# Attention scores without rotation from queries and keys in two parts: three float32r passes in place of one float32 product

## The chip, the cores and the metric

The kernel runs on one core of one Trainium2 chip. The metric is the device time of one execution in microseconds (us), the median of three runs. "float32r" below is the type F32R of the code: a four-byte type whose products the kernel uses wherever it carries a number as a coarse part ("hi") plus the rest ("lo").

## The reference

One inference step of four layers: a state-space layer, a pooling layer, a latent-attention layer, and a second state-space layer. The change lies in the attention layer alone. There 384 tokens (128 of the prompt, 256 of the sample) attend with 16 heads; the sample tokens also see 128 cached context tokens. Per head:

```
q_nope, q_pe = split((rmsnorm(q_a) @ wq_b) per head, 128 + 64)
k_nope, v    = split((ckv_n @ wkv_b) per head, 128 + 128)
s = einsum('bqhd,bkhd->bhqk', q_nope, k_nope) + einsum('bqhr,bkr->bhqk', q_pe, k_pe)
p = softmax(s * 192 ** -0.5)
o = einsum('bhqk,bkhd->bqhd', p, v)
```

The first product of `s` (128 features, not rotated) is what the change computes in another way. The second (64 rotated features) stays.

## The kernel before, in words

Nearly all weight products are taken in three float32r passes: both operands are split into hi (a copy rounded to float32r, on ScalarE) and lo (operand minus hi, on VectorE), and hi·hi, hi·lo and lo·hi are added up in one PSUM bank. The helper `split` (L145 to L147) does the two steps on a tile, `unit` (L131) and `unit2` (L776) on weights that arrive by DMA: `whi` and `wlo`. A few products are plain float32, among them both score products and the product of weights and values.

In `mla` (L588) the 16 heads run in a loop (L768 to L773) that is skewed by one head: `scores(h + 1)` is written ahead of `values(h)`. `scores(h)` builds the head's queries (L712 to L714: six passes, 384 columns, into a bank of the pool `acc`) and copies them to SBUF as `qn` on ScalarE (L716); builds its keys (L719 to L721: three passes, 512 columns) and copies them as `kn` on VectorE (L723); then, for three tiles T of 128 queries, takes the unrotated product (L729) and the rotated one (L730) into a bank of the pool `sp`. Tiles 0 and 2 are of the sample and see 384 keys; tile 1 is of the prompt and sees 128. Tile 1 writes the last 128 columns of the bank that holds tile 0. Each tile then gets its maximum (L733), `-scale` times it (L734), the exponential on ScalarE (L735), the reciprocal of its sum (L736) and the product with it (L737), which gives `P`.

`values(h)` transposes P in seven pieces (L752) into two banks, `tp` and `ad`, copies these out as `PT` on ScalarE (L755) and VectorE (L757), multiplies with the values `V` (L762, L763), multiplies with the gate (`pr`), and splits the result into `ph` and `pl`. Every fourth head `vals4` builds V for four heads in twelve passes (L698 to L700). Between the two, `beside()` (L771) splits two weight units of the next layer ahead of time and stores their lo parts to DRAM (L1024): `raw` in, `whi` on ScalarE, `wlo` on VectorE, `lod` out.

The order in which each engine meets its instructions is not that of the code: the Tile framework schedules the recorded instructions by their dependences and its own costs, so an edit in one place can move others. Once built, the order is fixed, and each engine works it off in turn. Tiles of one tag in a pool with `bufs=2` alternate between two buffers; with `bufs=1` the next writer waits for the last reader.

Of the kernel before, what the change touches and what calls it, by code (L numbers as in the profile page):

```python
# [9 lines left out]
F32 = mybir.dt.float32  # L10
F32R = mybir.dt.float32r
# [9 lines left out]
NT = 384  # L21
# [9 lines left out]
class Net:  # L31
# [556 lines left out]
    def mla(self, l, side, end, beside):  # L588
        nc, tc, A = self.nc, self.tc, self.A
        v = nc.vector  # L590
        scale = 192.0 ** -0.5
        with ExitStack() as outer:
# [25 lines left out]
            with tc.tile_pool(name="mp", bufs=1) as mp:  # L618
# [27 lines left out]
                for k in range(4):  # L646
                    ps = self.bank(self.tp, "tp")
# [20 lines left out]
                for n in range(2):  # L668
                    pss = [self.bank(self.acc, "acc") for _ in range(3)]
                    self.prod_b(pss, A["mla_wqp"][n], 1, qh, ql)  # L670
                    for T in range(3):
                        o = qp[:, T, n * 512:(n + 1) * 512]
# [4 lines left out]
                for k in range(8):  # L677
                    ps = self.bank(self.tp, "tp")
# [25 lines left out]
            def scores(h):  # L704
# [5 lines left out]
                for k in range(2):  # L710
# [1 line left out]
                    nc.tensor.matmul(ps, wh[:, c], qh[:, k, :], start=k == 0, stop=False)  # L712
                    nc.tensor.matmul(ps, wh[:, c], ql[:, k, :], start=False, stop=False)
                    nc.tensor.matmul(ps, wl[:, c], qh[:, k, :], start=False, stop=k == 1)  # L714
                qn = wk.tile([128, NT], F32, name="qn", tag="qn")
                nc.scalar.copy(out=qn, in_=ps)  # L716
                ps = self.bank(self.acc, "acc")
                c = slice(w0 + 256, w0 + 384)
                nc.tensor.matmul(ps, wh[:, c], ch, start=True, stop=False)  # L719
                nc.tensor.matmul(ps, wh[:, c], cl, start=False, stop=False)  # L720
                nc.tensor.matmul(ps, wl[:, c], ch, start=False, stop=True)  # L721
                kn = wk.tile([128, 512], F32, name="kn", tag="kn")
                v.tensor_copy(out=kn, in_=ps)  # L723
                hp = slice(64 * (h % 2), 64 * (h % 2) + 64)
                P = wk.tile([128, 3, NT], F32, name="P", tag="P")
                pa, pb = self.bank(self.sp, "sp"), self.bank(self.sp, "sp")
                for T, o, ks in ((0, pa[:, :384], slice(128, 512)), (1, pa[:, 384:], slice(0, 128)), (2, pb[:, :384], slice(128, 512))):
                    ts_ = slice(T * 128, (T + 1) * 128)
                    nc.tensor.matmul(o, qn[:, ts_], kn[:, ks], start=True, stop=False)  # L729
                    nc.tensor.matmul(o, qpT[hp, h // 2, ts_], kpT[hp, ks], start=False, stop=True)  # L730
                    n = ks.stop - ks.start
                    mx = self.work.tile([128, 3], F32, name="mx", tag="mx", bufs=6)
                    v.reduce_max(out=mx[:, 0:1], in_=o, axis=AX.X)  # L733
                    v.tensor_scalar(out=mx[:, 0:1], in0=mx[:, 0:1], scalar1=-scale, scalar2=None, op0=OP.mult)  # L734
                    nc.scalar.activation(out=P[:, T, :n], in_=o, func=AF.Exp, scale=scale, bias=mx[:, 0:1], accum_out=mx[:, 1:2])  # L735
                    v.reciprocal(out=mx[:, 2:3], in_=mx[:, 1:2])  # L736
                    v.tensor_scalar(out=P[:, T, :n], in0=P[:, T, :n], scalar1=mx[:, 2:3], scalar2=None, op0=OP.mult)  # L737
# [796 lines left out]
```

## Time and profile before

| | us |
|---|---|
| median of three runs | 1810.89 (1810.05 to 1817.27) |
| profiled execution | 1812.23 |
| its span, first to last instruction | 1810.4 |
| heads of the attention, 1073 to 1237 us of the span | 164 |

In the profile PE is TensorE with its matmuls, PEld its weight loads, DVE VectorE, ACT ScalarE, SP the engine whose queue issues the DMAs. A float32 product stands in the trace as two matmul rows with two weight loads, a float32r pass as one of each; a row with x2 or x4 merges neighbours. The ends of matmuls are modelled, so the cost of a matmul is read from its start to the start of the next, not from its duration.

### The profile page before, as it was taken

The page shows a single profiled execution, that of the slowest core. Times are in us where ns is not written, and L with a number is a line of the kernel's source. Part 1 is how long each engine was busy: PE and PEld are TensorE (multiplying, and loading weights), DVE is VectorE, ACT ScalarE, POOL GpSimd, SP SyncE. Part 2 cuts the span into 40 slices and gives each one's busy share as a digit, 9 for nine tenths or more (in the row PEclk, how much of TensorE's full clock was granted, in tenths as well). Part 3 has the DMA queues.
Part 4 walks back from the last instruction along what each step waited for, and adds up shares of the span by engine and source line. Part 5 has one row for each costly group of instructions (what it writes and reads, how often), then busy time and mean ns, then how long its engine had stood idle before and what let it go on. Part 6 is the DMA issues. An engine that isn't in the chain of part 4 may idle for free.

```text
span 1810.4 us, 29493 instructions
## 1 busy us (share of the span) xinstructions
PE 1686.1 (93%) x10928; PEld 1318.4 (73%) x10928; DVE 1254.9 (69%) x3149; ACT 978.3 (54%) x1588; POOL 5.4 (0%) x16
## 2 busy tenths in 40 slices
PE   4999999998999998999998999999899999899998
PEld 1464454654799977999887885657678778689986
DVE  7699876787476567888867737763439978656435
ACT  2653487636654455655546555642354777754322
POOL 0000000000000000000000000000000000000000
PEclk7999999997899998999998999999999999799999
DMA  8337767654577664655563566732567754567552
GB/s 311 98 119 240 228 182 220 195 180 137 166 252 231 193 205 135 188 162 163 179 218 113 186 205 229 239 127 82 181 226 226 227 182 140 166 232 213 172 165 72
DMA packets 174831, 334.30 MB, mean 185 GB/s; under 512 B 78528, under 2 KB 101856, under 8 KB 174688
## 3 DMA queue, kind: packets, MB, share of 16 engines
q1 hardware_dynamic: 165728, 319.84, 55.6%
q10 hardware_dynamic: 8960, 12.59, 2.1%
q8 instruction: 86, 1.41, 0.3%
q14 instruction: 57, 0.47, 0.1%
HBM read 279.54 MB, written 52.82 MB: 184 GB/s over the span
## 4 chain that ended last, share of the span: by engine, by line
PE 72%; DVE 9%; ACT 9%; DMA 6%; issue 3%; SPq 0%; ACTq 0%; DVEq 0%
PE acc L175 6%; PE acc L177 6%; PE acc L176 6%; PE sp L1122 4%; PE acc L829 4%; PE acc L830 4%; PE acc L831 4%; PE acc L213 3%; PE acc L159 3%; PE acc L160 3%; PE acc L161 3%; PE acc L204 3%; ACT Eq L1188 3%; DMA adw<-in_ada_w 2%; PE adps L99 2%
## 5 line engine op out<-in xcount | busy, mean ns | idle before, releaser
L51 DVE TENSOR_TENSOR wlo<-raw,whi 128x1024 fp32r<-128x1024 f32 (+2 forms) x234 | 281.2, 1204 | 246.3 <-ACT whi L138 229.0
L138 ACT CAST whi<-raw 128x1024 fp32r<-128x1024 f32 x246 | 257.6, 1050 | 315.2 <-PE acc L177 130.0
L51 DVE TENSOR_TENSOR Pr<-E,Tb 128x256 f32<-128x256 f32 (+1 forms) x504 | 173.9, 354 | 9.3 <-ACT E L1131 3.3
L159 PE MATMUL acc<-hh,whi 128*128 128x384 f32 x512 | 177.3, 347 | 0.2
L161 PE MATMUL acc<-hh,wlo 128*128 128x384 f32 x512 | 174.3, 340 | 0.3 <-DVE wlo L51 0.2
L160 PE MATMUL acc<-hl,whi 128*128 128x384 f32 x512 | 174.3, 340 | 0.0
L829 PE MATMUL acc<-y,whi 128*128 128x384 f32 x448 | 152.7, 345 | 8.1 <-ACT y L146 5.8
L831 PE MATMUL acc<-y,wlo 128*128 128x384 f32 x448 | 152.0, 340 | 1.0 <-DVE wlo L51 1.0
L830 PE MATMUL acc<-y,whi 128*128 128x384 f32 x448 | 152.7, 342 | 0.1
L175 PE MATMUL acc<-whi,ph 128*128 128x512 f32 x384 | 152.5, 397 | 0.0
L176 PE MATMUL acc<-wlo,ph 128*128 128x512 f32 x384 | 151.4, 394 | 0.0
L177 PE MATMUL acc<-whi,pl 128*128 128x512 f32 x384 | 151.3, 394 | 0.0
L51 DVE TENSOR_TENSOR E<-R,E 128x128 f32<-128x128 f32 (+1 forms) x504 | 123.1, 254 | 31.5 <-ACT E L1125 25.2
L51 DVE TENSOR_TENSOR R<-Pr 128x128 f32<-128x128 f32 (+1 forms) x504 | 123.7, 255 | 5.8
L159 PEld LDWEIGHTS acc<-hh,whi 128*128 128x128 f32 x512 | 97.1, 190 | 5.2 <-issue 2.0
L204 PE MATMUL acc<-h,raw 128*128 128x384 f32 x256 | 98.8, 516 | 0.0
L161 PEld LDWEIGHTS acc<-hh,wlo 128*128 128x128 f32 x512 | 96.8, 189 | 2.1 <-DVE wlo L51 0.9
L160 PEld LDWEIGHTS acc<-hl,whi 128*128 128x128 f32 x512 | 97.1, 190 | 1.0 <-issue 0.3
L99 PE MATMUL adps<-adw,scond 128*32 128x256 f32 x768 | 70.6, 422 | 27.7 <-DMA adw<-in_ada_w 27.3
L213 PE MATMUL acc<-raw,h 128*128 128x512 f32 x192 | 95.8, 617 | 0.0
L829 PEld LDWEIGHTS acc<-y,whi 128*128 128x128 f32 x448 | 84.6, 190 | 11.6 <-ACT y L146 7.1
L831 PEld LDWEIGHTS acc<-y,wlo 128*128 128x128 f32 x448 | 84.9, 190 | 2.2 <-DVE wlo L51 1.6
(285 smaller groups left out, 3261.6 us busy)
## 6 DMA issues: line engine op xcount, KB each, us to landing
adw<-in_ada_w SPq DMA_DIRECT2D x96, 512.0 KB
raw<-in_s_glu SPq DMA_DIRECT2D x64, 512.0 KB
raw<-in_s_wu SPq DMA_DIRECT2D x48, 512.0 KB
raw<-in_s_wz SPq DMA_DIRECT2D x40, 512.0 KB
raw<-in_s_wo SPq DMA_DIRECT2D x32, 512.0 KB
yq<-yd SPq DMA_DIRECT2D x64, 192.0 KB
lod<-wlo SPq DMA_DIRECT2D x24, 512.0 KB
wlo<-lod SPq DMA_DIRECT2D x24, 512.0 KB
```

The costliest lines, as they stand in the source:

```text
L51: return self.nc.vector.tensor_tensor(out=out, in0=a, in1=b, op=op)
L138: nc.scalar.copy(out=hi, in_=raw)
L159: nc.tensor.matmul(ps, h, xh[:, kk, :ncol], start=i == 0, stop=False)
L160: nc.tensor.matmul(ps, h, xl[:, kk, :ncol], start=False, stop=False)
L161: nc.tensor.matmul(ps, l, xh[:, kk, :ncol], start=False, stop=i == n - 1)
L175: nc.tensor.matmul(ps, xh[:, kk, xs], h, start=kk == 0, stop=False)
L176: nc.tensor.matmul(ps, xh[:, kk, xs], l, start=False, stop=False)
L177: nc.tensor.matmul(ps, xl[:, kk, xs], h, start=False, stop=kk == 2 * nu - 1)
L204: self.nc.tensor.matmul(ps, w[:, k * 128:(k + 1) * 128], x[:, k, :], start=k == 0, stop=k == 7)
L829: self.nc.tensor.matmul(ps, h, y[:, 0, k], start=u == 0 and k == 0, stop=False)
L830: self.nc.tensor.matmul(ps, h, y[:, 1, k], start=False, stop=False)
L831: self.nc.tensor.matmul(ps, l, y[:, 0, k], start=False, stop=u == 1 and k == 7)
```

## The change

`qn` and `kn` become pairs of float32r tiles, made by `split`: hi on ScalarE, lo on VectorE, both read from the PSUM bank. The unrotated product of each tile is three passes, each with a weight load of its own; the rotated product stays float32. The four tiles have one buffer each, where `qn` and `kn` had two. The lines behind the edit move by two (L733 becomes L735, and so on); the two copies now appear under the helper's lines, L146 and L51.

```diff
-                qn = wk.tile([128, NT], F32, name="qn", tag="qn")
-                nc.scalar.copy(out=qn, in_=ps)
+                qn = [wk.tile([128, NT], F32R, name="qn", tag=f"qn{i}", bufs=1) for i in range(2)]
+                self.split(*qn, ps)
...
-                kn = wk.tile([128, 512], F32, name="kn", tag="kn")
-                v.tensor_copy(out=kn, in_=ps)
+                kn = [wk.tile([128, 512], F32R, name="kn", tag=f"kn{i}", bufs=1) for i in range(2)]
+                self.split(*kn, ps)
...
-                    nc.tensor.matmul(o, qn[:, ts_], kn[:, ks], start=True, stop=False)
+                    nc.tensor.matmul(o, qn[0][:, ts_], kn[0][:, ks], start=True, stop=False)
+                    nc.tensor.matmul(o, qn[0][:, ts_], kn[1][:, ks], start=False, stop=False)
+                    nc.tensor.matmul(o, qn[1][:, ts_], kn[0][:, ks], start=False, stop=False)
                     nc.tensor.matmul(o, qpT[hp, h // 2, ts_], kpT[hp, ks], start=False, stop=True)
```

The scheduler orders the attention anew; outside it the engines' orders are as before. Two places matter. The first is TensorE in head 3 (the heads counted from 0), from the end of its keys on. Before:

```order
L721 MATMUL acc<-ch,wlo 128x512
L752 MATMUL tp<-ident,P 128x128
L752 MATMUL ad<-ident,P 128x128
L729 MATMUL sp<-kn,qn 128x384
L730 MATMUL sp<-kpT,qpT 128x384
L729 MATMUL sp<-kn,qn 128x384
L730 MATMUL sp<-kpT,qpT 128x384
L752 MATMUL tp<-ident,P 128x128 x3
L752 MATMUL ad<-ident,P 128x128 x2
L762 MATMUL acc<-PT,V 128x2x128 x2
```

With the change, the same place (L729 to L731 are the three passes, L732 the rotated product, L754 the transposes, L764 the product with the values):

```order
L721 MATMUL acc<-ch,wlo 128x512
L754 MATMUL tp<-ident,P 128x128
L754 MATMUL ad<-ident,P 128x128
L729 MATMUL sp<-kn,qn 128x384 x2
L754 MATMUL tp<-ident,P 128x128 x3
L754 MATMUL ad<-ident,P 128x128 x2
L730 MATMUL sp<-kn,qn 128x384
L731 MATMUL sp<-kn,qn 128x384
L732 MATMUL sp<-kpT,qpT 128x384
```

The hi·hi passes of tiles 0 and 2 now stand together, the last five transposes have moved in front of the other passes, and the product with the values comes after the second group of L730 to L732 instead of right behind the transposes.

The second place is VectorE in the same head, around the copy of the keys. Before:

```order
L737 TENSOR_SCALAR P<-P,mx 128x128
L51 TENSOR_TENSOR pl<-pr,ph 128x384
L723 COPY kn<-acc 128x512
L736 RECIPROCAL mx<-mx 128x1
L51 TENSOR_TENSOR wlo<-raw,whi 128x1024
L737 TENSOR_SCALAR P<-P,mx 128x384
```

With the change:

```order
L739 TENSOR_SCALAR P<-P,mx 128x128
L51 TENSOR_TENSOR qn<-acc,qn 128x384
L51 TENSOR_TENSOR wlo<-raw,whi 128x1024
L738 RECIPROCAL mx<-mx 128x1
L51 TENSOR_TENSOR pl<-pr,ph 128x384
L739 TENSOR_SCALAR P<-P,mx 128x384
L51 TENSOR_TENSOR kn<-acc,kn 128x512
```

In this head the lo part of the keys stands behind a weight split of 1024 columns (`wlo`), which before came after the copy of the keys.

## Rows read from the trace of the kernel before

**Rows 1.** The page, busy time and share of the span of each engine.

```profile
PE 1686.1 (93%) x10928; PEld 1318.4 (73%) x10928; DVE 1254.9 (69%) x3149; ACT 978.3 (54%) x1588; POOL 5.4 (0%) x16
```

**Rows 2.** Busy time by stretch: all heads; head 3; a head with vals4. Columns as headed.

```profile
core 0: us, PE busy (x) PEld busy (x) DVE busy (x) ACT busy (x) POOL busy (x), PEclk, DMA share, GB/s
1073.00:1237.00 164.00, 150.47 (x625) 97.31 (x624) 118.00 (x291) 91.22 (x197) 0.00 (x0) 0.99 0.58 192
...
1100.75:1110.53 9.78, 8.66 (x39) 5.46 (x38) 7.96 (x18) 5.28 (x12) 0.00 (x0) 1.00 0.61 194
...
1119.86:1132.42 12.56, 11.77 (x52) 7.81 (x51) 9.01 (x23) 9.44 (x20) 0.00 (x0) 1.00 0.40 126
```

**Rows 3.** Timeline of TensorE through head 3: start, duration, instruction [idle before].

```profile
1102.33 0.40 PE L721 MATMUL acc<-ch,wlo 128*128 128x512 f32 x1
1102.57 0.27 PE L752 MATMUL tp<-ident,P 128*128 128x128 f32 x1
1102.68 0.27 PE L752 MATMUL ad<-ident,P 128*128 128x128 f32 x1
1103.61 0.88 PE L729 MATMUL sp<-kn,qn 128*128 128x384 f32 x2 [0.66 <-DVE mx L736]
1104.42 0.91 PE L730 MATMUL sp<-kpT,qpT 64*128 64x384 f32 x2
1105.26 0.91 PE L729 MATMUL sp<-kn,qn 128*128 128x384 f32 x2
1106.10 0.91 PE L730 MATMUL sp<-kpT,qpT 64*128 64x384 f32 x2
1106.94 0.55 PE L752 MATMUL tp<-ident,P 128*128 128x128 f32 x3
1107.32 0.38 PE L752 MATMUL ad<-ident,P 128*128 128x128 f32 x2
1108.16 1.13 PE L762 MATMUL acc<-PT,V 128*128 128x256 f32 x4 [0.46 <-ACT PT L755]
1109.13 0.38 PE L729 MATMUL sp<-kn,qn 128*128 128x128 f32 x2
1109.44 0.49 PE L730 MATMUL sp<-kpT,qpT 64*128 64x128 f32 x2
...
1110.53 0.42 PE L712 MATMUL acc<-qh,whi 128*128 128x384 f32 x1
1110.79 0.34 PE L713 MATMUL acc<-ql,whi 128*128 128x384 f32 x1
1110.96 0.34 PE L714 MATMUL acc<-qh,wlo 128*128 128x384 f32 x1
```

**Rows 4.** Groups of VectorE's instructions, 1072 to 1238 us: busy, mean ns | idle before.

```profile
L51 DVE TENSOR_TENSOR wlo<-raw,whi 128x1024 fp32r<-128x1024 f32 x26 | 31.7, 1218 | 4.9 <-ACT whi L138 2.8 <-PE acc L161 2.1
L723 DVE COPY kn<-acc 128x512 f32<-128x512 f32 x16 | 11.0, 688 | 3.6 <-PE acc L721 3.6
L51 DVE TENSOR_TENSOR pr<-acc,sz 128x384 f32<-128x384 f32 x16 | 8.9, 554 | 5.1 <-PE acc L763 4.8
L51 DVE TENSOR_TENSOR wlo<-raw,whi 128x512 fp32r<-128x512 f32 x4 | 2.7, 682 | 0.0
```

**Rows 5.** Groups of ScalarE's instructions, the same stretch.

```profile
L755 ACT COPY PT<-tp 128x512 f32<-128x512 f32 x16 | 9.4, 589 | 8.7 <-PE tp L752 8.7
L716 ACT COPY qn<-acc 128x384 f32<-128x384 f32 x16 | 7.6, 476 | 4.9 <-PE acc L714 4.8
```

**Rows 6.** Who TensorE waited for, 1072 to 1238 us: total, times, longest.

```profile
PE sp L729 <- DVE mx L736: 4.0, 6, 0.7
...
PE acc L762 <- ACT PT L755: 2.8, 6, 0.5
```

**Rows 7.** Timeline of VectorE in head 3, around the copy of the keys.

```profile
1102.77 0.69 DVE L723 COPY kn<-acc 128x512 f32<-128x512 f32 x1
...
1103.44 1.21 DVE L51 TENSOR_TENSOR wlo<-raw,whi 128x1024 fp32r<-128x1024 f32 x1
1104.57 0.42 DVE L737 TENSOR_SCALAR P<-P,mx 128x384 f32<-128x384 f32 x1
```

## The prediction, on record before the changed kernel ran

> **What bounds the kernel now.** First the page: TensorE is busy 93% of the span, no other engine over 69% [rows 1]. That is an average of four layers; the change touches only the loop over heads, so next the busy time by stretch. The loop takes 164 us, in which PE is busy 150.5, DVE 118.0, ACT 91.2, at a granted clock of 0.99, which is the higher level, 2.4 GHz [rows 2]. PE is the bound there, but not without gaps, and VectorE is the runner-up.
>
> Then one head in the timeline [rows 3]; by start to start it gives every price. A float32r pass over 384 columns takes 0.17 us behind another such pass (1110.79 to 1110.96), but 0.26 when a float32 product stands before it (1110.53 to 1110.79): changing from float32 to float32r costs 0.09. A float32 score product over 384 columns takes 0.81 (1103.61 to 1104.42) or 0.84 (1105.26 to 1106.10), one over 128 columns 0.31 (1109.13 to 1109.44). A transpose takes 0.11 (1102.57 to 1102.68). The head has two gaps. Between the second transpose, whose time is over by about 1102.8, and 1103.61 PE waits some 0.8 us. The row names a DVE reciprocal; what stands in DVE just before that is the copy of the keys, 1102.77 to 1103.46 [rows 7], and that is what L729 needs. The second gap is 0.46 at L762: the transposes have only just been done, and their copy PT takes 0.59 on ACT [rows 3, 5]. The waits summed over the loop show the same two, 4.0 and 2.8 us in six heads each [rows 6]; small, because modelled ends of matmuls cover part of each gap.
>
> **The change, part by part.**
>
> *Large tiles.* Two per head, 32 in all: a float32 product of 0.81 and one of 0.84 give way to three passes each at 0.17, 0.51. That saves 0.30 + 0.33 = 0.63 per head, 16 x 0.63 = 10.1 us.
>
> *Small tile.* One per head, 0.31 against three passes over 128 columns, which the trace before does not have. From below a third of the pass over 384, 0.06, from above the transpose of 128 columns, 0.11: 0.18 to 0.33 for three. I take 0.25, nearer to the transpose, since that has the same columns. Saves 0.06, 1.0 us in all (2.1 saved to 0.3 lost).
>
> *Changes of type.* The rotated product stays float32 and sits between the passes, and the scheduler puts transposes between them too. Counted along PE's order, a float32r pass follows a float32 product or a transpose 24 times in the loop before and 72 times after. 48 more at 0.09 [rows 3] cost 4.3 us. From below nothing, where PE stands waiting anyway; from above all of it. I take all.
>
> PE's own work so falls by 10.1 + 1.0 - 4.3 = 6.8 us (between 5.5 and 12.2).
>
> A rule of the skill speaks against the size of the first term. The rows show a float32 product at 0.84, or nearly five passes. The Trainium skill, "FP8 and Floating Point Precision", section TensorE Precision Notes, says that true float32 is four passes through the array. At four passes of 0.17 the product would cost 0.68 and the three passes save one, 32 x 0.17 = 5.4 us instead of 10.1; the sum would be 2.1. The trace disagrees on the time, so the row decides, and the sum is made by it.
>
> *VectorE.* Added: the lo part of the queries, 384 columns from PSUM, by the nearest row (pr) 0.55, 16 x 0.55 = 8.9 us. The lo part of the keys takes the place of the copy of the keys, 0.69 against 0.68 for a subtraction of 512 columns [rows 4]: nothing. DVE comes to 126.9 us in a loop of some 157, 81%. *ScalarE.* The queries' copy stays (0.48); the keys' hi part is new, 512 columns from PSUM as in PT, 0.59, 16 x 0.59 = 9.4 us [rows 5]: 100.6 of 157, 64%. Neither becomes the bound by its sum, so both cost nothing beside a PE that is busy over 90%; what they can cost is lateness.
>
> *The wait for the keys.* Before: end of L721, one DVE copy, L729. After: end of L721, hi on ACT (0.59 against 0.69 for the copy: L729 starts no later), then lo on DVE (0.69) before L730 may start. PE's new order covers that: behind the two L729 (0.26 + 0.17) stand five transposes (5 x 0.11), 0.98 us of work against 0.69. And because the transposes now precede the long passes, PT is copied under the 2.5 us of L730 to L732, and the 0.46 wait at L762 goes. Against that, VectorE works in order. Along its order a weight split of 1.21 us stands between the head's queries and its keys' lo part in 4 of 16 heads (3, 5, 7, 11); in head 3 before, it stood behind the copy and the scaling of P at 1104.57 was late by it, but nobody needed that until 1106.94 [rows 3, 7]. Now the transposes in front of L730 do. Estimate: of the 12 heads without vals4, the nine others gain 0.46 each, 4.1 us; three lose 1.21 - 0.46 = 0.75, 2.3 us; and ACT's queue puts the exponential of tile 2 and the cast of `ph` before the keys' cast in several heads, which I let eat the remaining 1.8. In the heads with vals4 its twelve passes lie beside the split, and only PE's own work counts [rows 2]. So the waits come to 0, between -4.1 and +9.4 (the whole new ACT link open in every head).
>
> *Single buffers.* The cast of the next head's queries must wait until the small tile of this head has been read. In most heads that lies before L712 on PE anyway; where it was moved behind L719, the cast waits about 1 us, but L729 waits for the keys, which come later still. Cost 0, and if it shows, it is inside the +9.4.
>
> *Next layer's weights.* The SP queue issues the same loads and `lod` stores in another order. They are read a layer later; cost 0.
>
> Sum: -6.8. The profiled execution took 1812.2, its span 1810.4, and lies 1.3 above the median of the runs, so on its own count it becomes 1805.4, and in medians 1810.9 - 6.8 = 1804.1.
>
> **The rivals.**
>
> A. *The second link is open.* PE saves 6.8, but the keys' extra link through ACT shows in every head: +9.4, net +2.6, 1813.5. For it: the wait before L729 is there today. Against: the five transposes that now stand in it.
>
> B. *Slower: VectorE's queue ends the wait.* In each of the 12 heads without vals4 the keys' lo part and the scaling of P stand behind a weight split (1.21) on top of the ACT link (0.59): 12 x 1.80 = 21.6, less 6.8, +14.8, 1825.7. It decides from the point at which heads wait 1.0 us more each than today (6.8 + 9.1 over 16). For it: DVE at 81%, strictly in order, 26 such splits in the loop [rows 4]. Against: only 4 heads have the split at that place.
>
> C. *More than the forecast.* The changes of type fall into waits, and PT's wait goes in all 12 heads: -12.2 - 5.5 = -17.7, 1793.2; half of the way there, -12.2, 1798.7. For it: of the 48 added changes some 20 are transposes followed by an L729 that waits for the keys anyway. Against: it wants ACT and DVE on time throughout.
>
> D. *The passes here cost more than 0.17.* If a float32 product is four passes and the rest is the price of the place (short groups, weights of their own for every tile), then three passes cost 0.63 of 0.84 and save 0.21: 32 x 0.21 = 6.7 instead of 10.1, in all -3.4, 1807.5. Against: the groups of six passes at 0.17 have new weights in every pass too. The rule of the Trainium skill above points to this side.
>
> **How the numbers follow.** Forecast 0.48, C 0.20, D 0.12, A 0.13, B 0.07. A measurement of this kernel can tell about 0.5% from no change, 9.1 us. Forecast and D lie within that, between -9 and -2; of the forecast's share I put 0.05 beyond -9, so faster is 0.20 + 0.05 = 0.25. Slower is B, 0.07, and the worst of A, 0.01: 0.08. The rest, 0.67, is within 0.5%. The range reaches down to the half of C, 1798, and up past A to 1815; the rest of C and B, about 2 in 10, is left out.
>
> **What would show each step right or wrong.** The loop over heads should last some 157 us instead of 164, and no other stretch change. L729 to L731 should stand 0.17 apart within a group, 0.26 at its head, and groups of 384 columns end after 0.6 us. L764 should wait for PT in few heads. If the loop is no shorter and PE's waits name the lo part of `kn` or P, A or B has it; then the heads with the weight split in front must be the longest. If the passes lie 0.21 apart, D has it. A gain over 9 us with no wait left at L764 speaks for C. The forecast is wrong if the loop grows, or if the time moves outside the loop.

## The result, and the profile after

The changed kernel takes 1823.68 us (median of 15 runs, 1815.84 to 1834.84) against 1810.05 us (15 runs, 1805.94 to 1817.27) for the kernel before on the same chip: ratio 1.0077, 95% interval 1.0057 to 1.0096. It is slower by some 0.8%, where 1804.1 us had been predicted, with 0.08 on slower. The profiled execution took 1816.74 us (span 1814.9), so it is one of the shorter of the fifteen; the mean granted clock of TensorE in it is 0.962; over the fifteen it goes from 0.969 in the shortest run to 0.950 in the longest.

The page's line of busy times, against [rows 1]: every engine has a little more to do, and TensorE is no less busy.

```profile
PE 1690.2 (93%) x10976; PEld 1329.1 (73%) x10976; DVE 1262.5 (70%) x3165; ACT 986.2 (54%) x1604; POOL 5.4 (0%) x16
```

Busy time by stretch, with the columns of [rows 2]: the loop over heads; 2 us in it in which TensorE waits; the 13.7 us behind that wait.

```profile
1067.30:1239.30 172.00, 157.77 (x675) 110.46 (x673) 125.90 (x307) 99.35 (x213) 0.00 (x0) 0.93 0.54 183
1136.50:1138.50 2.00, 0.50 (x4) 0.17 (x2) 2.00 (x5) 1.91 (x5) 0.00 (x0) 1.00 0.06 22
1138.50:1152.20 13.70, 13.68 (x35) 9.49 (x36) 8.63 (x24) 5.72 (x13) 0.00 (x0) 0.50 0.76 258
```

The loop takes 171.9 us, 7.8 more than the 164.1 of before, and PE is busy 157.8 us instead of 150.5. The granted clock of the loop has fallen from 0.99 to 0.93. The third row shows how: 13.7 us at 0.50, which is the lower level, 1.2 GHz. The clock's record has two such stretches inside the loop, 13.7 us from 1138.5 and 10.2 us from 1182.9, and a third, of 3.4 us, lies over its end; the loop before has only the one at its end. At half speed half of the time is lost: 12.8 us against 1.7.

Ahead of each of the two TensorE had stood still: 1.51 us up to 1138.5 and 2.08 us up to 1183.2. The timeline of TensorE around the first (start, duration, instruction, idle before):

```profile
1136.39 0.40 PE L721 MATMUL acc<-ch,wlo 128*128 128x512 f32 x1
1136.62 0.27 PE L754 MATMUL tp<-ident,P 128*128 128x128 f32 x1
1136.73 0.27 PE L754 MATMUL ad<-ident,P 128*128 128x128 f32 x1
1138.52 1.26 PE L729 MATMUL sp<-kn,qn 128*128 128x384 f32 x2 [1.51 <-ACT kn L146]
1139.58 0.52 PE L730 MATMUL sp<-kn,qn 128*128 128x384 f32 x1
1139.90 0.52 PE L731 MATMUL sp<-kn,qn 128*128 128x384 f32 x1
1140.35 1.65 PE L732 MATMUL sp<-kpT,qpT 64*128 64x384 f32 x2
```

The pass waits for the keys' hi part, `kn` by ScalarE (L146). Behind the wait passes follow each other by 0.32 us (1139.58 to 1139.90) instead of 0.17, and the rotated product takes 1.57 (1140.35 to 1141.92) instead of 0.84. ScalarE's timeline shows why `kn` is late:

```profile
1135.63 0.48 ACT L146 CAST qn<-acc 128x384 fp32r<-128x384 f32 x1 [0.34 <-PE sp L730]
1136.59 1.04 ACT L138 CAST whi<-raw 128x1024 fp32r<-128x1024 f32 x1 [0.48 <-PE acc L720]
1137.54 0.36 ACT L737 ACTIVATE P<-sp,mx 128x128 f32<-128x128 f32 x1
1137.80 0.19 ACT L737 ACTIVATION_READ_ACCUMULATOR P<-sp,mx 128x1 f32 x1
1137.89 0.57 ACT L146 CAST kn<-acc 128x512 fp32r<-128x512 f32 x1
```

The last product of the keys starts at 1136.39, and its cast at 1137.89: a weight cast of 1.04 us and an exponential stand in front of it in an engine that works strictly in order. At 1180.73 the same weight cast stands there again, with two exponentials behind it; the keys' cast starts at 1182.59, and TensorE waits 2.08 us:

```profile
1183.22 0.69 PE L729 MATMUL sp<-kn,qn 128*128 128x384 f32 x1 [2.08 <-ACT kn L146]
```

The waits of the loop, against [rows 6] (total, times, longest):

```profile
PE sp L729 <- ACT kn L146: 6.1, 5, 2.1
PE tp L754 <- DVE P L739: 4.9, 5, 2.2
PE acc L764 <- ACT PT L757: 1.4, 3, 0.5
```

At full clock the passes look as foreseen. The first two tiles of an early head, against [rows 3]:

```profile
1078.22 0.44 PE L729 MATMUL sp<-kn,qn 128*128 128x384 f32 x1
1078.50 0.33 PE L730 MATMUL sp<-kn,qn 128*128 128x384 f32 x1
1078.67 0.34 PE L731 MATMUL sp<-kn,qn 128*128 128x384 f32 x1
1078.94 0.91 PE L732 MATMUL sp<-kpT,qpT 64*128 64x384 f32 x2
1079.78 0.44 PE L729 MATMUL sp<-kn,qn 128*128 128x384 f32 x1
```

Passes are 0.17 apart, but from L729 to the next L729 it is 1.56 us, against 1.65 to 1.68 for two float32 products in [rows 3] (1103.61 to 1105.26, 1104.42 to 1106.10). A tile saves some 0.1 us, not 0.3. On VectorE and ScalarE the new work has the durations and the sum foreseen, against [rows 4, 5]:

```profile
L51 DVE TENSOR_TENSOR kn<-acc,kn 128x512 fp32r<-128x512 f32 x16 | 10.9, 682 | 0.7 <-ACT kn L146 0.7
L51 DVE TENSOR_TENSOR qn<-acc,qn 128x384 fp32r<-128x384 f32 x16 | 8.8, 553 | 1.3 <-ACT qn L146 1.0
```

```profile
L146 ACT CAST kn<-acc 128x512 fp32r<-128x512 f32 x16 | 9.4, 588 | 1.0 <-PE acc L721 1.0
```

### The profile page after: what moved, and what is told of

The parts are those of the page before. It is cut to its first block, busy times and chain, and to the rows that moved or that the text cites. A ratio compares the mean times of both kernels' runs of the same rounds, so it can differ in the third digit from the quotient of the medians.

```text
span 1814.9 us, 29615 instructions
## 1 busy us (share of the span) xinstructions
PE 1690.2 (93%) x10976; PEld 1329.1 (73%) x10976; DVE 1262.5 (70%) x3165; ACT 986.2 (54%) x1604; POOL 5.4 (0%) x16
## 4 chain that ended last, share of the span: by engine, by line
PE 69%; ACT 10%; DVE 9%; DMA 8%; issue 3%; SPq 0%; ACTq 0%; DVEq 0%
PE acc L175 6%; PE acc L177 6%; PE acc L176 6%; PE sp L1124 4%; PE acc L831 4%; PE acc L832 4%; PE acc L833 4%; PE acc L159 3%; PE acc L161 3%; DMA adw<-in_ada_w 3%; PE acc L160 3%; PE acc L213 3%; ACT Eq L1190 3%; PE acc L204 2%; PE adps L99 2%
## 5 line engine op out<-in xcount | busy, mean ns | idle before, releaser
L51 DVE TENSOR_TENSOR wlo<-raw,whi 128x1024 fp32r<-128x1024 f32 (+2 forms) x234 | 281.1, 1204 | 247.2 <-ACT whi L138 232.1
L51 DVE TENSOR_TENSOR Pr<-E,Tb 128x256 f32<-128x256 f32 (+1 forms) x504 | 173.3, 353 | 9.3 <-ACT E L1133 3.3
L51 DVE TENSOR_TENSOR E<-R,E 128x128 f32<-128x128 f32 (+1 forms) x504 | 122.5, 253 | 31.5 <-ACT E L1127 25.2
L51 DVE TENSOR_TENSOR R<-Pr 128x128 f32<-128x128 f32 (+1 forms) x504 | 123.0, 254 | 5.7
```

What stands on the lines that cost most here:

```text
L51: return self.nc.vector.tensor_tensor(out=out, in0=a, in1=b, op=op)
```

## The experiments

The theories, numbered as in the expectations below: 1, the keys' parts wait behind other work in an in-order queue, TensorE stands still, and the clock falls to half; 2, the split's load on VectorE and ScalarE costs by itself; 3, the passes and what stands between them cost more than was counted; 4, the stretches at half clock have nothing to do with the waits. Theory 5 came up on the way. Each kernel was compared with the kernel before on its own chip. "Loop" is from the first query pass of head 0 to the first pass of the output product in the one profiled execution; "lost" is what the lower clock took of it, half of the time at 0.50.

| kernel | median us (runs) | ratio to before [95%] | loop us | lost us | longest wait in the loop, us |
|---|---|---|---|---|---|
| before | 1810.05 (15) | 1 | 164.1 | 1.7 | 1.0 |
| after | 1823.68 (15) | 1.0077 [1.0057, 1.0096] | 171.9 | 12.8 | 2.1 |
| two buffers | 1831.31 (6) | 1.0092 [1.0059, 1.0124] | 167.1 | 6.8 | 2.1 |
| keys on VectorE | 1841.29 (5) | 1.0149 [1.0125, 1.0173] | 196.0 | 30.2 | 2.0 |
| passes only | 1819.55 (11) | 1.0028 [1.0010, 1.0046] | 166.3 | 6.4 | 1.5 |
| split work only | 1823.72 (6) | 1.0052 [1.0033, 1.0071] | 169.8 | 5.1 | 1.6 |
| keys of the head before | 1808.65 (12) | 0.9985 [0.9968, 1.0002] | 159.9 | 1.7 | 1.8 |
| idle filled | 1820.19 (8) | 1.0041 [1.0026, 1.0056] | 172.1 | 0.7 | 1.1 |
| rotated first, three passes | 1812.72 (12) | 1.0004 [0.9987, 1.0022] | 161.9 | 7.8 | 1.6 |
| rotated first, float32 | 1803.14 (6) | 0.9938 [0.9916, 0.9961] | 153.0 | 1.7 | 1.4 |
| keys first, three passes | 1811.12 (12) | 0.9994 [0.9970, 1.0017] | 154.6 | 2.6 | 1.1 |
| keys first, float32 | 1801.17 (7) | 0.9933 [0.9908, 0.9957] | 152.1 | 1.7 | 0.7 |
| before, 128 rows | 1799.86 (6) | 0.9934 [0.9909, 0.9960] | 150.5 | 0.0 | 1.9 |
| after, 128 rows | 1804.35 (11) | 0.9960 [0.9941, 0.9979] | 156.0 | 6.8 | 2.5 |
| before, padded | 1802.96 (7) | 0.9948 [0.9927, 0.9969] | 152.6 | 1.7 | 2.1 |
| keys first, padded, float32 | 1792.25 (6) | 0.9880 [0.9858, 0.9901] | 141.0 | 1.6 | 0.7 |
| keys first, padded, three passes | 1800.10 (6) | 0.9921 [0.9896, 0.9946] | 148.7 | 3.1 | 1.2 |

(The wait before the last head's transposes, 2.1 to 2.7 us at the loop's end in nearly every kernel, is left out of the last column.)

The loop and the loss are those of one execution each; the mean granted clock is on record for every run. (1 - clock) x span is half of the time at 0.50 in a whole execution, the measure of "lost" for all of it. It is 73 us on average for after, and 61 to 63 us for before on the four chips of the experiments (12 to 23 runs each; on the chip of after the clocks of before aren't on record). The 11 to 12 us between them are the 11.1 us between the two profiled loops, and what is left of the time is the same: 1750 us for after, 1750 to 1752 for before. So the clock accounts for what after loses in its runs as a whole, as far as before on those chips stands for before on this one.

One reservation holds for most rows. The scheduler orders the loop anew for each kernel. TensorE keeps its order, instruction by instruction, in the two kernels with 128 rows and in "before, padded", and in "two buffers" but for 16 of 672 places. In "split work only", "passes only", "keys of the head before", "idle filled" and "keys on VectorE" some 250 to 350 of these places hold another instruction, so these kernels show what an edit and its new order do together.

### Two buffers

```
-                qn = [wk.tile([128, NT], F32R, name="qn", tag=f"qn{i}", bufs=1) for i in range(2)]
+                qn = [wk.tile([128, NT], F32R, name="qn", tag=f"qn{i}", bufs=2) for i in range(2)]
...
-                kn = [wk.tile([128, 512], F32R, name="kn", tag=f"kn{i}", bufs=1) for i in range(2)]
+                kn = [wk.tile([128, 512], F32R, name="kn", tag=f"kn{i}", bufs=2 - i) for i in range(2)]
```

> Both parts of the queries and the hi part of the keys get two buffers again (the lo part of the keys stays at one, for space). Theory 1 (long waits for the keys' hi part in ScalarE's queue let TensorE's clock fall to its lower level; buffers have no part in it): as with the change, 1816 to 1830 us, still one or two stretches of the heads' loop at a granted clock of 0.5. Rival 'single buffers' (the next head's cast of the queries waits for the last reader of the old ones, and the keys' cast stands behind it): 1806 to 1813, no such stretch.

No gain: 1.0092 against 1.0077. The order hardly moves and the waits are like those of after: the longest is 2.08 us again, with 13.7 us at half clock behind it; an earlier one, of 1.53 us, has none. The single buffers aren't the cause.

### The keys' hi part on VectorE

```
-                self.split(*kn, ps)
+                v.tensor_copy(out=kn[0], in_=ps)
+                self.tt(kn[1], ps, kn[0].bitcast(F32), OP.subtract)
```

> The keys' hi part is made on VectorE, as the copy of the keys was before, and ScalarE has no part in the keys any more; VectorE does 16 x 0.69 us more. Theory 1: the waits of 1.5 and 2.1 us behind ScalarE go, the clock holds, 1806 to 1815 us. Rival 'VectorE is too full': VectorE's queue is late instead, 1818 to 1835. Rival 'the passes themselves': 1816 to 1826.

The worst of all, far outside theory 1's range and beyond the rival's: the loop grows to 196 us, with six stretches at 0.50 and 30.2 us lost to them. The longest waits are for VectorE's `kn` (1.54 and 1.84 us) and, on ScalarE's queue, for the cast of the queries (1.65 and 2.01 us). Taking the keys' cast out of one queue and putting it into the other cures nothing.

### The passes only

```
-                qn = [wk.tile([128, NT], F32R, name="qn", tag=f"qn{i}", bufs=1) for i in range(2)]
-                self.split(*qn, ps)
+                qn = wk.tile([128, NT], F32R, name="qn", tag="qn")
+                nc.scalar.copy(out=qn, in_=ps)
...
-                kn = [wk.tile([128, 512], F32R, name="kn", tag=f"kn{i}", bufs=1) for i in range(2)]
-                self.split(*kn, ps)
+                kn = wk.tile([128, 512], F32R, name="kn", tag="kn")
+                v.tensor_copy(out=kn, in_=ps)
...
-                    nc.tensor.matmul(o, qn[0][:, ts_], kn[1][:, ks], start=False, stop=False)
-                    nc.tensor.matmul(o, qn[1][:, ts_], kn[0][:, ks], start=False, stop=False)
+                    nc.tensor.matmul(o, qn[:, ts_], kn[:, ks], start=False, stop=False)
+                    nc.tensor.matmul(o, qn[:, ts_], kn[:, ks], start=False, stop=False)
```

> The lo parts are left out: one float32r copy of queries (ScalarE) and keys (VectorE), two buffers each, as before, and the three passes all read it. TensorE does the changed work, the other engines the old one. Theory 1: no long waits, no lower clock, and TensorE's own work about as before (three passes and two changes of type, 0.7 us, against 0.84 in large tiles, more in small ones): 1806 to 1814 us. Rival 'the passes themselves': 1816 to 1826. If the first term of the prediction held as it stood: 1800 to 1805.

With no lo parts and the keys on VectorE as before, three passes are still not faster than float32: 1.0028. Theory 1's "no long waits, no lower clock" is missed, and so is its range. One wait of 1.52 us for `kn` has a stretch of 10.2 us at half clock behind it. Even without the lost time the loop is only 2.5 us shorter than before without its own (166.3 - 6.4 against 164.1 - 1.7), where 6.8 had been predicted: the first sign that the passes save less. (The loop doesn't explain the median here: the profiled execution took 1646 us outside it in before and 1653 in this one.)

### The split's work only

```
                 nc.scalar.copy(out=qn, in_=ps)
+                ql_ = wk.tile([128, NT], F32, name="ql", tag="ql", bufs=1)
+                self.tt(ql_, ps, qn, OP.subtract)
...
                 v.tensor_copy(out=kn, in_=ps)
+                kh = wk.tile([128, 512], F32, name="kh", tag="kh", bufs=1)
+                nc.scalar.copy(out=kh, in_=ps)
```

> The kernel before, its scores in float32, with the split's extra work alone: one more subtraction of 384 columns per head on VectorE and one more copy of 512 columns per head on ScalarE, whose results nothing reads (a program with the same output). Theory 1 (waits for the keys' parts behind other work in an engine's queue, then a fall of the clock to half): the copies lengthen the queues, but the scores need only what they needed before, so the loop takes 164 to 168 us and the time is 1810 to 1815 us; single waits over 1.2 us with a stretch at half clock behind them would be the load's own part in it. Rival 2 (the load on VectorE and ScalarE as such makes the loop longer, whoever waits for it): the loop is at 168 to 174 us and the time at 1816 to 1826 us. Rival 3 (the passes themselves cost more than float32): the time of the kernel before, 1810 us.

Theory 1's number (1810 to 1815) is missed; the loop and the time are those of theory 2. TensorE has the same instructions as before, though in a new order (248 of 624 places differ), nobody reads the extra work, and still the kernel loses 0.5%. The way is the one of theory 1, as far as the trace shows it. In one head the keys' copy on VectorE now stands behind the extra subtraction, and the first float32 product waits, with half clock behind it (1.32 us for L734 instead of 0.84):

```profile
1145.13 0.27 PE L756 MATMUL ad<-ident,P 128*128 128x128 f32 x1
1147.04 0.88 PE L733 MATMUL sp<-kn,qn 128*128 128x384 f32 x2 [1.64 <-DVE mx L740]
1147.86 1.40 PE L734 MATMUL sp<-kpT,qpT 64*128 64x384 f32 x2
```

```profile
1144.49 0.55 DVE L51 TENSOR_TENSOR ql<-acc,qn 128x384 f32<-128x384 f32 x1
1146.21 0.68 DVE L725 COPY kn<-acc 128x512 f32<-128x512 f32 x1
```

Three more waits of 1.56 to 1.64 us in this loop have no half clock behind them. The two theories aren't rivals then: the load, with the order that it brings, costs by waits, even where the sums of busy time (124.5 and 100.1 of 169.8 us) leave room.

### The keys of the head before

```
-                kn = [wk.tile([128, 512], F32R, name="kn", tag=f"kn{i}", bufs=1) for i in range(2)]
+                kn = [wk.tile([128, 512], F32R, name="kn", tag=f"kn{i}", bufs=2) for i in range(2)]
                 self.split(*kn, ps)
+                kn, st["kn"] = st.get("kn", kn), kn
```

> The changed kernel with passes that read the keys' two parts of the head before (two buffers each), so that no pass has to wait for the split of its own head's keys; all split work stays (this leaves the reference: 15 heads are scored with another head's keys). Theory 1: no wait over 1.2 us at the passes, no stretch at half clock within the loop, loop 155 to 160 us against 171.9 us in the changed kernel and 164.1 us in the kernel before; time 1803 to 1812 us. Rival 2 (load of the split) and rival 3 (passes and switches of type cost more than counted): the loop stays at 166 to 172 us and the time at 1816 to 1826 us.

All the split's work and all passes stay, the wait for the own keys is gone (and the order is new): 0.9985 instead of 1.0077, loop 159.9, no half clock before the loop's end. That is theory 1's range, at its upper end for the loop. Against its expectation one wait of 1.76 us remains at a pass, for an exponential of P, and has no half clock behind it.

### TensorE's idle time filled

```
+                    if T == 0:
+                        for _ in range(4):
+                            nc.tensor.matmul(pb, wh[:, c], ch, start=True, stop=True)
```

> The changed kernel with four more passes of 512 columns per head, put ahead of the scores: they write a bank that tile 2 opens afterwards, nothing reads them, and they fill TensorE's wait for the keys. They add 16 x 4 x 0.23 = 14.7 us of TensorE work, of which some 8 us lie in waits. Theory 1 (the clock falls because TensorE waits): no stretch at half clock within the loop; loop 160 to 170 us, so not longer than the changed kernel's 171.9 us in spite of more work; time 1812 to 1823 us. Rival 4 (the stretches at half clock have nothing to do with the waits): stretches of 10 to 14 us stay, loop 176 to 184 us, time 1826 to 1836 us.

64 more passes at 0.23 us are 14.7 us more work on TensorE, and the loop is as long as after's (172.1, a little over theory 1's 160 to 170). The row by stretch has a clock of 1.00 instead of 0.93:

```profile
1070.18:1242.33 172.15, 162.15 (x738) 115.67 (x737) 126.71 (x307) 99.67 (x213) 0.00 (x0) 1.00 0.54 183
```

The waits in front of the passes are down to 0.3 us and less, since the filling waits in their stead, at most 1.1 us. It isn't this execution alone: over its eight runs (1 - clock) x span is 58 us on average, against 73 for after. The stretches at half clock hang on the waits, as theory 1 has it; theory 4's ranges, 176 to 184 us for the loop and 1826 to 1836 in all, are missed.

### The rotated product first, in three passes and in float32

```
-                    nc.tensor.matmul(o, qn[0][:, ts_], kn[0][:, ks], start=True, stop=False)
+                    nc.tensor.matmul(o, qpT[hp, h // 2, ts_], kpT[hp, ks], start=True, stop=False)
...
-                    nc.tensor.matmul(o, qpT[hp, h // 2, ts_], kpT[hp, ks], start=False, stop=True)
+                    nc.tensor.matmul(o, qn[0][:, ts_], kn[1][:, ks], start=False, stop=True)
```

This is the version in three passes; in float32 the one product without rotation closes the sum.

> The rotated float32 product, which does not need the split keys, opens each tile's sum, and the three passes follow. Behind the keys' own passes TensorE then has two rotated products, 1.7 us of work, instead of a wait. Theory 1: no wait over 1 us in the loop except at its end, no stretch at the lower clock, and float32 stands next to float32, so fewer changes of type: 1794 to 1806 us. Rival 'the passes themselves' (the three passes with their changes of type cost TensorE more than the float32 product): 1814 to 1826, whatever the clock does.

> The kernel before, all in float32, with one thing moved: the rotated product opens each tile's sum and the product without rotation closes it. It tells how much of the equal time of the version with the rotated product first in three passes comes from covering the waits and how much from the passes. Theory 1: the waits of the kernel before are 0.7 to 1.0 us and no clock is lost behind them, so at most their sum of some 4 us is to be had: loop 160 to 164 us, time 1805 to 1811 us. Rival 3 (passes no cheaper than float32): like the three passes with the rotated product first, ratio 0.999 to 1.002 to the kernel before.

In three passes it brings after back to the time of before, no further, between the two ranges. Two waits of 1.58 and 1.47 us remain, both for an exponential on ScalarE: the first stands behind a weight cast that itself waited 3.83 us for its DMA, the second behind another weight cast. In float32 the same move gains 0.6%, more than either side expected, and its loop of 153.0 us is 11 us shorter than before, more than all covered waits together (the loop of before is idle for 13.5 us, this one for 10.5). TensorE itself had become cheaper by 8 us with the same instructions. The order put two rotated products, and then two others, next to each other:

```profile
1119.36 1.55 PE L729 MATMUL sp<-kpT,qpT 64*128 64x384 f32 x4
1120.84 1.56 PE L730 MATMUL sp<-kn,qn 128*128 128x384 f32 x4
```

Halves of a float32 product then follow by 0.32 us, those over 64 rows too, and by 0.43 and 0.41 around each change from 64 to 128 rows. This gave theory 5: a change of rows costs some 0.2 us, and the prices of [rows 3] have it in them.

### 128 rows for the rotated product

```
-                    nc.tensor.matmul(o, qpT[hp, h // 2, ts_], kpT[hp, ks], start=False, stop=True)
+                    nc.tensor.matmul(o, qpT[:, h // 2, ts_], kpT[:, ks], start=False, stop=True)
```

> The kernel before with the rotated product over all 128 rows in place of one half of 64 (this leaves the reference: each head's score takes in the rotated part of its neighbour too). All is float32, and the order of the two products is as before; what goes is the change between products over 128 and over 64 rows. The version with the rotated product first showed halves of a float32 product 0.32 us apart where like follows like, and 0.42 us apart at each change. Theory 5 (the change of rows costs some 0.10 us on either side, 0.2 us per product): a product takes 0.64 us in place of 0.84 us in the run of four, 3.33 us per head become 2.6 us, and the loop is at 152 to 157 us, the time at 1798 to 1805 us. Rival (what costs is any change of product, or the rotated product first wins by covered waits alone): products stay at 0.81 to 0.84 us, loop 162 to 166 us, time 1808 to 1814 us.

> The changed kernel with the rotated product over all 128 rows in place of one half of 64 (this leaves the reference in the same way). Between passes and rotated product the type still changes each time, the rows no more. Theory 5, if a change of type costs its 0.1 us whether or not the rows change with it: three passes and one rotated product stay at 1.56 us and the time stays at the changed kernel's, 1816 to 1826 us. Rival (the two changes add up): 1.56 us become 1.36 us, the loop falls by 32 x 0.2 = 6.4 us and the time to 1810 to 1817 us. The waits for the keys stay as they were in both.

Theory 5 holds. In the order of before, which TensorE keeps instruction by instruction, float32 throughout, the timeline now reads:

```profile
1100.79 0.88 PE L729 MATMUL sp<-kn,qn 128*128 128x384 f32 x2 [0.66 <-DVE mx L736]
1101.51 0.81 PE L730 MATMUL sp<-kpT,qpT 128*128 128x384 f32 x2
1102.15 0.81 PE L729 MATMUL sp<-kn,qn 128*128 128x384 f32 x2
1102.80 0.81 PE L730 MATMUL sp<-kpT,qpT 128*128 128x384 f32 x2
1103.44 0.49 PE L752 MATMUL tp<-ident,P 128*128 128x128 f32 x3
...
1105.58 0.39 PE L729 MATMUL sp<-kn,qn 128*128 128x128 f32 x2
1105.80 0.39 PE L730 MATMUL sp<-kpT,qpT 128*128 128x128 f32 x2
1106.02 0.60 PE L762 MATMUL acc<-PT,V 128*128 128x256 f32 x2
```

A product behind another takes 0.64 or 0.65 us in place of 0.81 to 0.84, the four 2.65 in place of 3.33, and a product of the small tile 0.22 (1105.58 to 1105.80); the loop falls by 13.6 us, to a little under the range. In the changed kernel, whose order stays as well, the expectation that the change of type keeps its price was wrong, and the rival's was right and too small:

```profile
1095.21 0.52 PE L730 MATMUL sp<-kn,qn 128*128 128x384 f32 x1
1095.58 0.33 PE L731 MATMUL sp<-kn,qn 128*128 128x384 f32 x1
1095.75 0.81 PE L732 MATMUL sp<-kpT,qpT 128*128 128x384 f32 x2
1096.10 0.63 PE L730 MATMUL sp<-kn,qn 128*128 128x384 f32 x1
1096.57 0.34 PE L731 MATMUL sp<-kn,qn 128*128 128x384 f32 x1
...
1098.31 0.27 PE L730 MATMUL sp<-kn,qn 128*128 128x128 f32 x1
1098.42 0.27 PE L731 MATMUL sp<-kn,qn 128*128 128x128 f32 x1
```

From float32r to float32 it is 0.17 (1095.58 to 1095.75), the price of the pass alone. In the other direction the pass is entered at 1096.10, while the float32 product still runs; but from one L731 to the next it is 0.99, which is 0.64 + 2 x 0.17 and nothing more. A change of type at equal rows costs nothing here. (The last two rows are of the small tile: its passes stand 0.11 apart.) The waits for `kn` stay (6.4 us in all, longest 2.1), yet this kernel loses only 6.8 us to the clock, in four stretches of 3.4 us each; why they are shorter here isn't shown.

### The keys' product ahead of the queries'

```
+                nc.tensor.matmul(ps, wh[:, c], ch, start=True, stop=False)
...
                 nc.tensor.matmul(ps, wh[:, c], qh[:, k, :], start=k == 0, stop=False)
...
-                nc.tensor.matmul(ps, wh[:, c], ch, start=True, stop=False)
```

> Three passes with the rotated product first, and the keys' product ahead of the queries' in each head, so that the keys' split has the six query passes (1.05 us) and the rotated products as cover. Theory 1 (waits behind ScalarE's queue, then half clock): no wait over 1.2 us in the loop, no stretch at half clock but at its end, loop 151 to 157 us, time 1800 to 1808 us. Rival 2 (load of the split): the loop is at 160 to 164 us and the time at 1810 to 1815 us, as with the rotated product first alone.

> The same order (keys' product ahead of the queries', rotated product first), the scores all in float32. Against the same order in three passes it tells what the three passes are worth where neither waits. From like products at 0.64 us and three passes at 0.52 us, the passes would save 32 x 0.12 = 3.8 us and 16 x 0.0 us on the small tiles, less what 48 more changes of type take (here 2 per head in place of 1, 0.1 us each: 1.6 us), so some 2 us: Theory 1 and 5 say 1799 to 1806 us here and a difference under 4 us between the two. Rival 2 (load of the split costs by itself): this one is faster than the three passes by 6 to 10 us.

In the profiled executions both loops are where theory 1 has them, 154.6 and 152.1 us. The medians aren't: three passes stay at 0.9994, float32 gains 0.7%. The twelve runs of the three passes reach from 1797.86 to 1818.43, and the profiled one, at 1809.36 us, came to its loop only at 1080.7 us (before: 1073.0). The float32 version wins by some 10 us in the median, which is theory 2's range, and by 2.5 us in the loop, which is theory 1's. The clocks of all runs say what the 10 us are: (1 - clock) x span is 72 us on average for the three passes and 60 for float32, and what is left of the time is the same, 1739 and 1740 us. Where in the longer runs the clock is lost, one profile can't tell.

### Padded rows: the change of rows taken away for good

```
+            kz = pp.tile([128, 2, 512], F32, name="kz")
+            nc.gpsimd.memset(kz, 0.0)
...
+                    v.tensor_copy(out=kz[hp, i, :], in_=kpT[hp, :])
...
-                    nc.tensor.matmul(o, qpT[hp, h // 2, ts_], kpT[hp, ks], start=False, stop=True)
+                    nc.tensor.matmul(o, qpT[:, h // 2, ts_], kz[:, h % 2, ks], start=False, stop=True)
```

> The kernel before with the rotated product over all 128 rows and the same result: the rotated keys lie in two copies, each with zeros in the half that belongs to the neighbour, so the neighbour's queries add nothing. It costs one clearing on GpSimd and two copies of 64 x 512 ahead of the loop (under 1.5 us on VectorE). Theory 5 (change of rows, 0.2 us at each change): as with the neighbour's part left in, loop 149 to 154 us, ratio 0.990 to 0.997. Rival (that gain came from other numbers, or the copies give it back): ratio 0.998 to 1.002.

> Float32, padded rows, the rotated product first and the keys' product ahead of the queries': Theory 1 and 5 say that both gains are there, less what both gave by the same means (like beside like): loop 145 to 150 us, ratio 0.987 to 0.993. Rival (the order won only by putting like beside like, which padding makes worthless): the same as the padded kernel in the order of before, loop 149 to 153 us, ratio 0.991 to 0.996.

> The same order with padded rows, in three passes. Products alone: 32 large ones save 0.64 - 0.51 = 0.13 us each, 16 small ones lose 0.33 - 0.22 = 0.11 us, so 2.4 us less TensorE work than in float32. Theory 1 (the split costs only by waits, and these are covered here): 0 to 4 us faster than float32 in the same order. Rival 2 (the split's load on VectorE and ScalarE costs whatever the order): 4 to 12 us slower than float32 in the same order, with waits of over 0.6 us that the float32 version does not have.

Padding alone takes 0.5% off the kernel before (0.9948). With the keys first, float32, it is the best version found: 1792.25 us, 0.9880, its loop even shorter than expected. The order's gain doesn't vanish with the change of rows, so it was covered waits as well (idle time in the loop 8.0 us, against 18.3 in the order of before with padded rows). The same in three passes is 0.4% above it (1800.10 against 1792.25; the two intervals overlap by a hair, at 0.990). The two loops by stretch, float32 first:

```profile
1079.24:1220.23 140.99, 133.02 (x623) 98.84 (x621) 115.15 (x291) 90.54 (x196) 0.00 (x0) 0.99 0.65 220
```

```profile
1076.01:1224.74 148.73, 133.39 (x671) 106.34 (x669) 123.02 (x307) 97.00 (x212) 0.00 (x0) 0.98 0.62 208
```

TensorE is busy for the same 133 us; 7.4 of the 7.7 us between them are idle time (8.0 against 15.3), most of it in the waits of the three passes:

```profile
PE tp L759 <- DVE P L744: 4.8, 3, 2.6
PE sp L734 <- ACT P L742: 4.7, 5, 1.1
PE acc L769 <- ACT PT L762: 4.5, 10, 0.6
```

In float32 the first two are 2.3 and 1.1 us. The rival was right on the size: where the keys no longer wait, P comes later instead. That the split's load delays it is argued from these names alone. Over all six runs of each the gap looks otherwise: the clock takes 69 us on average from the three passes and 59 from float32, and apart from that the three passes are 3 us shorter, close to the 2.4 us that their TensorE work should save. In the profiled pair only 1.5 us of the clock's share lie in the loop; where the rest lies in the other runs isn't shown.

## Why the prediction was wrong

Two steps failed: the size of what the passes save, and the wait for the keys, which was put at nothing and turned into lost clock.

*Large tiles* (-10.1): mis-sized. The step took 0.81 and 0.84 us as the price of a float32 product. That price holds a change between 64 and 128 rows, 0.2 us, which comes from the rotated product beside it and stays when the other product is split. Without it the product is 0.64 us, three passes are 0.51, and 32 x 0.13 = 4.2 us were to be had. The working even had the hint: the Trainium skill, "FP8 and Floating Point Precision", section TensorE Precision Notes, has true float32 as four passes, and four at 0.17 are 0.68. It was set aside because a row showed 0.84; with the rows equal the trace shows 0.64 and nearly agrees with it (over 128 columns it does not: 0.22 against four times 0.11). Another rule of the Trainium skill may bear on what the row held besides: "TensorEngine Tiling (Array Packing)", section Key Properties, says that changing the tiling mode drains TensorE, and gives no price. The change of rows cost 0.2 us here; that it is such a drain, no run shows. Rival D (three passes save 0.21) was nearer in size than the forecast, and right that the product holds a price of its place; but that price stays, and the passes took 0.17 as in the forecast.

*Small tile* (-1.0): wrong in sign. A float32 product over 128 columns is 0.22 us at equal rows, three passes are 0.33: a loss of 1.8 us over 16 heads.

*Changes of type* (+4.3): nothing of it. The 0.09 was misread from the trace of before. Ahead of the pass at 1110.53 stands a row that [rows 3] leave out:

```profile
1110.39 0.38 PE L763 MATMUL acc<-PT,V 128*128 128x128 f32 x2
```

From its start to the second pass at 1110.79 it is 0.40 us, the float32 product's 0.22 and the pass's 0.17 and nothing more; the pass is only entered early, while the product still runs. The version with 128 rows shows the same. By these prices the sum for TensorE was to be 4.2 - 1.8 = 2.4 us less, not 6.8.

*VectorE* and *ScalarE*: the sums were right (125.9 and 99.4 us busy, against 126.9 and 100.6 foreseen). That they "cost nothing beside a PE that is busy over 90%" was wrong: this work alone, with TensorE's instructions of before in a new order, costs 0.5%.

*The wait for the keys* (0, between -4.1 and +9.4): this is the step that failed most, in its first line, "L729 starts no later". The five transposes were to cover the lo part at L730, and no wait for it shows in the loop of after. The waits came one step earlier, at L729, for the hi part: in the two worst heads a weight cast of 1.04 us and one or two exponentials stand ahead of it in ScalarE's queue, and L729 waits 1.51 and 2.08 us. The working counted the weight splits in VectorE's queue and left ScalarE's an estimate of 1.8 us in all. The waits in sum hardly grew (idle 14.2 us against 13.5 in the loop), and the wait at PT fell as foreseen, from 2.8 to 1.4. But the idle time gathered into two long waits, and behind each the clock fell. The prediction had no term for that; it is 12.8 - 1.7 = 11.1 us, more than any of its other terms. With 0.7 us more idle time and some 4 us less busy time at full clock (157.8 - 12.8 against 150.5 - 1.7) it makes the 7.8 us by which the loop grew.

*Single buffers* and *next layer's weights* (0 each): right for the first, by the version with two buffers. For the second, the stretch behind the loop took 575.7 us against 573.3, of which 2.8 us are lost clock there; nothing points to the loads.

Rival B had the sign and, at 1825.7, nearly the time, but by luck, not by the cause: it wanted VectorE's queue and 1.8 us in twelve heads. Two waits behind ScalarE's queue and the clock did it.

What stays open: the median of the changed kernel lies 7 us above its profiled execution, and no trace shows the longer runs. Part of it is that this execution was quick elsewhere: it came to the loop 5.7 us sooner than the profiled one of before (1067.3 against 1073.0), though the engines' orders ahead of the loop are the same. Nor is it shown what decides whether a wait has half clock behind it, or what the extra work would cost in the old order.

## What to carry to other kernels

A price read between neighbours belongs to both: before a matmul's duration is taken as what its removal saves, look for a place in the trace where like follows like, and ask what of it stays with the neighbour. On an engine that works in order, look up what will stand ahead of the instruction that TensorE waits for, not the engine's busy share; and price a wait that grows with the clock that may fall behind it: here it did so behind 12 of 21 waits of 1.5 us and more. Ask of a single profile whether the clocks of the other runs bear it out. If halves of 64 rows alternate with products of 128 rows, zeros in the other half may be the cheapest change of all: here 0.5% alone, 1.2% with the keys first.

## What the runs showed of the hardware

- A change between products of 64 and of 128 rows cost 0.2 us each time (float32 over 384 columns: 0.84 us alternating, 0.64 us at equal rows). A change between float32r and float32 at equal rows cost nothing that the starts over 384 columns show.
- The granted clock of a busy loop fell to 0.50 (1.2 GHz) behind single waits of 1.5 to 2.1 us, for 3.4 to 13.7 us. Not behind every one: of 21 waits of 1.5 us and more in the loops of all profiled executions (the last head's transposes left out) 12 had such a stretch starting in them or close behind, 9 had none, the longest of these 2.46 us (after, 128 rows). In the padded three passes, and twice with the keys on VectorE, two waits of 0.8 to 1.1 us close to each other had one, and once (after, 128 rows) there was one with no wait over 0.8 us close ahead of it.
- Within such a stretch float32r passes over 384 columns were 0.32 us apart instead of 0.17, and TensorE counted as 100% busy (13.68 of 13.70 us): the busy share shows nothing of it, the clock does.
